# Attention output in transposed form, two heads in the two halves of TensorE's columns, and the softmax transposes one tile later

## The chip, the cores and the metric

The kernel runs on one core of a Trainium2 chip. The metric is device time in microseconds, the median of three runs. The engines spoken of are TensorE (PE; its weight loads are PEld), VectorE (DVE), ScalarE (ACT), GpSimd (POOL) and SyncE's DMA queue (SP).

## The reference, cut to what matters

One encoder block on 1024 tokens of width 1024. The change is inside the attention part; 8 heads of 64 columns each, neighbours of a 16 by 64 grid of tokens:

```python
z = rms_norm(x, norm_mix) @ w_in                      # u | q | k | v
q = rms_norm(q, q_norm) * (HD ** -0.5); k = rms_norm(k, k_norm)
s = einsum('bhcd,bhicjd->bhcij', q_r, k_nb) + bias    # 8 x 16 neighbours
pr = softmax(s);  y_attn = einsum('bhcij,bhicjd->bhcd', pr, v_nb)
x = x + concatenate([y_pool, y_attn]) @ w_out
x = x + expert_choice_ffn(...);  x = x + sigmoid(...) * rms_norm(...)
```

## The kernel before

Tokens are cut into 8 tiles of 128 (eight grid columns by 16 rows), so the neighbours of a tile lie in the tile itself and the ones beside it. Heads are worked in four pairs, 128 columns each. The attention loop runs over 32 tiles t = 8 pr + u, pair after pair. TensorE's order is the order in which the code issues it; in this stretch a scheduler orders the other engines.

`pair_block(t)` is a tile's projection: eight groups of three matmuls (L94, L96, L98 in the helper `mm3`) into `proj`, 384 columns wide. When the eighth is done, ScalarE squares q and k (L307) and copies v (L312), VectorE sums the squares (L309), GpSimd takes the root (L79, L80), and VectorE scales q and k into `qkn` (L313). Between the groups of one tile's projection stand steps of earlier tiles; `side_at(t)` lists them with the group ahead of which each is issued, and 8 means behind the last group:

- step 0: `score(t-3)`, six matmuls of two heads that use the upper and lower 64 rows of the array (L346): q hi and q lo with k hi, then q hi with k lo. VectorE adds the bias and takes the maximum (L351), ScalarE takes the exponential and the row sum (L353).
- steps 5 and 6: `turn_p(t-3, h)`, transposes of head h's exponentials (L361), brought to SBUF as `PT` by ScalarE (head 0) or VectorE (head 1). Step 6 also has `turn_qk(t-1)`, two transposes of `qkn` (L321); ScalarE writes the high part of k and then of q, VectorE the low parts (L327, L328). All tiles of k of a pair are in `kT`.
- steps 7 and 8: `blend(t-3, h)`, attention weights by v in full fp32 (L375): `PT` is the stationary operand, 64 columns of v move. Each such matmul is two instructions on TensorE (176 matmuls are 352 rows of the trace). After head 1 VectorE multiplies with the reciprocal of the row sums (L379, L380) into `ya`, token rows by head columns.

For a tile u the keys reach from tile u-1 to u+1 (`span`), so `score(t-3)` needs the k that `turn_qk(t-2)` writes, except at u = 7, the last tile of a pair.

From tile 4 on, step 3 also holds one piece of the pooling mixer. Weights of the next pair and of `w_out` are loaded and split (L88, L89, L85, L86) along the way. After the 32 tiles, `out_block(u)` multiplies pooling and attention output by `w_out`; it holds the last steps of the attention. `prep(u)` makes its operand `ct`: four transposes of `ya` (L462) into a PSUM buffer of tag t, then a split by ScalarE and VectorE. From block 3 on, the ranking for the experts runs on VectorE. Then 16 experts and a gate, which the change doesn't touch.

Of the kernel before, what the change touches and what calls it, by code (L numbers as in the profile page):

```python
# [10 lines left out]
F32 = mybir.dt.float32  # L11
# [4 lines left out]
ALU = mybir.AluOpType  # L16
# [3 lines left out]
P = 128  # L20
# [3 lines left out]
NU = 8  # L24
# [7 lines left out]
HD = 64  # L32
# [14 lines left out]
def block_kernel(ctx, tc, x, p, vecs, w_u_in, w_qkv, w_pool, bias_rows, w_out, w_router, w_gate, w_up,  # L47
                 w_down, w_ple_gate, w_ple_proj, norm_ffn, norm_ple_post, edge, consts, out):
    nc = tc.nc
    ACT, DVE, POOL, PE, SP = nc.scalar, nc.vector, nc.gpsimd, nc.tensor, nc.sync  # L50
# [8 lines left out]
    def pool(name, bufs, **kw):  # L59
        return tc.tile_pool(name=name, bufs=bufs, reuse_waits="tile", **kw)  # L60

    cp = ctx.enter_context(pool("consts", 1))
    tiny = ctx.enter_context(pool("tiny", 4))
# [4 lines left out]
    ident = cp.tile([P, P], F32, name="ident")  # L68
# [14 lines left out]
    def split(hi, lo, src, gain=None):  # L83
        if gain is None:
            ACT.activation(hi, src, AF.Copy)  # L85
            DVE.tensor_tensor(lo, src, hi.bitcast(F32), op=ALU.subtract)  # L86
            return
        ACT.activation(hi, src, AF.Copy, scale=gain)  # L88
        DVE.scalar_tensor_tensor(lo, src, gain, hi.bitcast(F32), op0=ALU.mult, op1=ALU.subtract)  # L89
# [37 lines left out]
    yas = [rawp["B"].tile([P, 4, 512], F32, tag="raw", name=f"ya_{i}") for i in range(2)]  # L127
# [4 lines left out]
    ps = ps_st.enter_context(pool("ps", 2, space=PSUM))  # L132
# [153 lines left out]
        PE.matmul(pp, w_pool_sb[:, g], Ug, start=True, stop=True)  # L286
        ACT.activation(Ug, pp, AF.Copy, scale=pscale[:, g:g + 1])

    vs, qs, qkns, sbs, PTs, pys, dens = {}, {}, {}, {}, {}, {}, {}
    bias_t = {}  # L290

    def load_bias(pr):
# [38 lines left out]
    def span(u):  # L331
        u0, u1 = max(u - 1, 0), min(u + 2, NU)
        return u0, u1, (u1 - u0) * P

    def score(t):
        pr, u = divmod(t, NU)
        u0, u1, n = span(u)
        b0 = 0 if u == 0 else 5 * P if u == NU - 1 else 2 * P
        q2 = qs[t]
        dens[t] = tiny.tile([P, 2], F32, tag="den", name=f"den_{pr}_{u}")  # L340
        ks = slice(u0 * P, u1 * P)
        pq = [ps.tile([P, 3 * P], F32, tag="s", name=f"s_{pr}_{u}_{h}") for h in range(2)]
        for a, b in ((0, 0), (1, 0), (0, 1)):
            for h in range(2):
                hs = slice(h * HD, (h + 1) * HD)
                PE.matmul(pq[h][:, :n], q2[hs, a], kT[hs, b, ks], start=(a + b == 0), stop=(b == 1))  # L346
        for h in range(2):
            pss = pq[h]
            sb = aw.tile([P, 3 * P], F32, tag="sb", name=f"sb_{pr}_{u}_{h}", bufs=4)
            nmx = tiny.tile([P, 1], F32, tag="nmx", name=f"nmx_{pr}_{u}_{h}")  # L350
            DVE.tensor_tensor_reduce(sb[:, :n], pss[:, :n], bias_t[pr][:, h, b0:b0 + n], -1.0, 3.0e38,  # L351
                                     ALU.add, ALU.min, nmx)
            ACT.activation(sb[:, :n], sb[:, :n], AF.Exp, bias=nmx, scale=-1.0, accum_out=dens[t][:, h:h + 1])  # L353
            sbs[t, h] = sb

    def turn_p(t, h):
# [9 lines left out]
            DVE.tensor_copy(PT[:, :n], pt[:, :n])  # L366
        PTs[t, h] = PT

    def blend(t, h):
        pr, u = divmod(t, NU)  # L370
        u0, u1, n = span(u)
        if h == 0:
            pys[t] = ps.tile([P, 2, HD], F32, tag="py", name=f"py_{pr}_{u}", bufs=1)
        for j in range(u1 - u0):
            PE.matmul(pys[t][:, h], PTs[t, h][:, j * P:(j + 1) * P],  # L375
                      vs[NU * pr + u0 + j][:, h * HD:(h + 1) * HD], start=(j == 0), stop=(j == u1 - u0 - 1))
        if h == 1:
            rd = tiny.tile([P, 2], F32, tag="rd", name=f"rd_{pr}_{u}")
            DVE.reciprocal(rd, dens[t])  # L379
            DVE.tensor_tensor(yas[u // 4][:, u % 4, pr * P:(pr + 1) * P].rearrange("p (a b) -> p a b", b=HD), pys[t],  # L380
                              rd[:, :, None].to_broadcast([P, 2, HD]), op=ALU.mult)

    wo = []

# [13 lines left out]
    NT = 4 * NU  # L398
# [9 lines left out]
    def side_at(t):  # L408
        sides = {}

        def at(i, f, *a):
            sides.setdefault(i, []).append(lambda: f(*a))
        if t == 0:
            at(4, turn_u, NU - 1)
        if t >= 3:
            at(0, score, t - 3)
            at(5, turn_p, t - 3, 0)
            at(6, turn_p, t - 3, 1)
            at(7, blend, t - 3, 0)
            at(8, blend, t - 3, 1)  # L420
        if 1 <= t <= NT:
            at(6, turn_qk, t - 1)
        return sides

    for t in range(NT):
        pr, u = divmod(t, NU)
# [22 lines left out]
    def prep(u):  # L449
        if u == 0:  # L450
            ow.tile([P, 2 * 16], F32, tag="gap", name="gap_ow", bufs=1)
        ct = ow.tile([P, 2, KD, P], F32R, tag="ct", name=f"ct_{u}")
        cts[u] = ct
        for i in range(2):
            usl = Us[i][:, :, PAD:PAD + S].rearrange("p g (r v c) -> p g v r c", v=NU, c=UC)[:, :, u]
            hi = ct[:, 0, 2 * i:2 * i + 2].rearrange("p g (r c) -> p g r c", c=UC)
            lo = ct[:, 1, 2 * i:2 * i + 2].rearrange("p g (r c) -> p g r c", c=UC)
            ACT.activation(hi, usl, AF.Copy)
            POOL.tensor_tensor(lo, usl, hi.bitcast(F32), op=ALU.subtract)
        pt = ps.tile([P, 4, P], F32, tag="t", name=f"yat_{u}", bufs=1)  # L460
        for k in range(4):
            PE.transpose(pt[:, k, :], yas[u // 4][:, u % 4, k * P:(k + 1) * P], ident)  # L462
        split(ct[:, 0, 4:8], ct[:, 1, 4:8], pt)

    def add_x(u, po, j):
        js = slice(j * 512, (j + 1) * 512)
# [199 lines left out]
    def open_route():  # L666
        nonlocal oc, w_r, affq, scr, sel
        oc = ctx.enter_context(pool("oc", 1, side="right"))
        both = oc.tile([P, 2, D], F32, tag="raw", name="both")
        scr, sel = both[:, 0], both[:, 1]  # L670
        w_r = sel[:, 0:KD * E].rearrange("p (k e) -> p k e", e=E)
        SP.dma_start(w_r, w_router[0].rearrange("(k p) e -> p k e", p=P))
        DVE.tensor_tensor(w_r, w_r, gfT[:, :, None].to_broadcast([P, KD, E]), op=ALU.mult)
        affq = sel[:, 128:128 + NU * 32].rearrange("p (u e) -> p u e", e=32)
        POOL.memset(affq, 0.0)
# [72 lines left out]
    load_x(0)  # L748
    load_x(1)
    prep(0)  # L750
    for u in range(NU):
        sides = {}

        def at(i, f, *a):
            sides.setdefault(i, []).append(lambda: f(*a))
        if u == 0:
            at(0, score, NT - 3)
            at(2, turn_p, NT - 3, 0)
            at(2, turn_p, NT - 3, 1)
            at(3, turn_qk, NT - 1)  # L760
            at(4, blend, NT - 3, 0)
            at(4, blend, NT - 3, 1)
            at(4, score, NT - 2)
            at(6, turn_p, NT - 2, 0)
            at(6, turn_p, NT - 2, 1)
            at(6, score, NT - 1)
            at(7, blend, NT - 2, 0)
            at(7, blend, NT - 2, 1)
            at(8, turn_p, NT - 1, 0)
            at(8, turn_p, NT - 1, 1)  # L770
        elif u < NU - 1:
            at(0, norm1, u - 1)
            at(2, turn_x1, u - 1, 0)
            at(2, turn_x1, u - 1, 1)
            at(4, route, u - 1)
        if u == 1:
            at(1, blend, NT - 1, 0)
            at(1, blend, NT - 1, 1)
        if u + 1 < NU:
            at(5, prep, u + 1)  # L780
        if u >= 1 and u + 1 < NU:
            at(0, load_x, u + 1)
        if u == 1:
            def swap():
                att.close()
                open_route()
                rawp["A"] = ctx.enter_context(pool("rawA", NRA, side="right"))
                load_side()
            at(2, swap)
        if u == 2:  # L790
            at(1, split_side, "pT")
            at(4, split_side, "pj")
            at(6, lambda: [load_chunk("A") for _ in range(NRA - 5)])
        if 3 <= u < NU - 1:
            at(6, rank_batch, *((0, 3) if u == 3 else (u - 1, 1)))
            for i in range(8):
                at(i, fill, 8)
        if u == NU - 1:
            at(1, turn_x1, u - 1, 0)
            at(1, turn_x1, u - 1, 1)  # L800
            at(1, norm1, u - 1)
            at(2, logits, u - 1, 0)
            at(3, logits, u - 1, 1)
            at(3, softmax, u - 1)
            at(5, rank_batch, 6, 1)
            for i in range(1, 8):
                at(i, fill, 8)
        run_block(out_block(u), sides)

    u = NU - 1  # L810
# [362 lines left out]
```

## Time and profile before

| | us |
|---|---|
| median of 3 runs | 1684.27 (1682.45 to 1686.49) |
| the profiled execution's own time | 1682.92 |
| its span | 1681.2 |
| TensorE busy | 1630.8 (97%) |
| VectorE busy | 1347.5 (80%) |
| ScalarE busy | 1153.9 (69%) |
| GpSimd busy | 169.1 (10%) |

The page's busy shares are averages over all stages. The attention tiles are the stretch from about 84 to 305 us; the output blocks end at about 437 us; the rest is the experts and the gate.

### The profile page before, as it was taken

To read this page: it belongs to the slowest core of one execution; us is meant where nothing else is said; L and a number is where in the kernel's file an instruction comes from. 1 tells how busy PE (TensorE), PEld (TensorE's weight loads), DVE (VectorE), ACT (ScalarE), POOL (GpSimd) and SP (SyncE) were. 2 spreads that over 40 slices of the span, in tenths; PEclk is the share of its full clock that TensorE was granted. 3 is DMA by queue.
4 is the path that set the end of the run, shared out by engine and by line. 5 is a ranking of instruction groups with operands and counts; after the bars stand their busy time and mean duration, and the time that the engine had idled before them with its cause. 6 is when DMAs were issued, how large, how long until landed. Compare 5 with 4: busy or idle time off the path is not lost.

```text
span 1681.2 us, 22945 instructions
## 1 busy us (share of the span) xinstructions
PE 1630.8 (97%) x8165; PEld 1368.0 (81%) x8165; DVE 1347.5 (80%) x1866; ACT 1153.9 (69%) x1471; POOL 169.1 (10%) x216
## 2 busy tenths in 40 slices
PE   8999998998899999999999999999999999999698
PEld 6889998886778888888888888888888888888587
DVE  4474555459879999999999999999999999999632
ACT  6254554432488888888888888888888888888431
POOL 1111112243310000000000000000000000000100
PEclk9999999999999999999999999999999999999799
DMA  6301201363699999999999999999999999996321
GB/s 187 116 29 33 66 26 51 92 204 97 216 365 373 401 371 400 377 368 408 373 391 385 367 403 377 378 399 369 399 378 367 410 370 392 386 368 242 106 98 59
DMA packets 129266, 470.54 MB, mean 280 GB/s; under 512 B 9600, under 2 KB 14720, under 8 KB 129152
## 3 DMA queue, kind: packets, MB, share of 16 engines
q1 hardware_dynamic: 122848, 445.80, 70.3%
q0 software_dynamic: 6304, 23.28, 5.3%
q8 instruction: 64, 1.05, 0.3%
q14 instruction: 50, 0.41, 0.1%
HBM read 448.00 MB, written 21.04 MB: 279 GB/s over the span
## 4 chain that ended last, share of the span: by engine, by line
PE 84%; DVE 7%; issue 4%; DMA 2%; POOL 1%; ACT 1%; SPq 0%; DVEq 0%; ACTq 0%; POOLq 0%
PE pu L94 7%; PE pu L96 7%; PE pu L98 7%; PE pg L94 6%; PE pg L96 6%; PE pd L96 6%; PE pd L94 6%; PE pg L98 6%; PE pd L98 6%; DVE both L581 3%; PE proj L94 2%; PE proj L98 2%; PE proj L96 2%; PE py L375 2%; PE pq L94 2%
## 5 line engine op out<-in xcount | busy, mean ns | idle before, releaser
L86 DVE TENSOR_TENSOR flo<-fraw,fhi 128x1024 fp32r<-128x1024 f32 x768 | 916.3, 1222 | 71.0 <-ACT fhi L85 33.5
L85 ACT ACTIVATE fhi<-fraw 128x1024 fp32r<-128x1024 f32 x768 | 809.4, 1061 | 192.6 <-PE pd L96 72.6
L94 PE MATMUL pd<-fhi,hidT 128*128 128x512 f32 x512 | 162.1, 398 | 0.0
L94 PE MATMUL pg<-fhi,xeT 128*128 128x512 f32 x512 | 159.2, 392 | 0.7 <-ACT xeT L85 0.7
L94 PE MATMUL pu<-fhi,xeT 128*128 128x512 f32 x512 | 159.2, 392 | 0.0
L96 PE MATMUL pd<-fhi,hidT 128*128 128x512 f32 x512 | 158.4, 390 | 0.0
L98 PE MATMUL pd<-flo,hidT 128*128 128x512 f32 x512 | 158.0, 390 | 0.0
L96 PE MATMUL pu<-fhi,xeT 128*128 128x512 f32 x512 | 158.0, 390 | 0.0
L96 PE MATMUL pg<-fhi,xeT 128*128 128x512 f32 x512 | 157.9, 389 | 0.0
L98 PE MATMUL pg<-flo,xeT 128*128 128x512 f32 x512 | 157.8, 389 | 0.0
L98 PE MATMUL pu<-flo,xeT 128*128 128x512 f32 x512 | 157.6, 389 | 0.0
L98 PEld LDWEIGHTS pd<-flo,hidT 128*128 128x128 f32 x512 | 96.1, 188 | 20.7
L96 PEld LDWEIGHTS pd<-fhi,hidT 128*128 128x128 f32 x512 | 96.1, 188 | 20.6
L96 PEld LDWEIGHTS pg<-fhi,xeT 128*128 128x128 f32 x512 | 96.0, 188 | 20.4 <-DVE xeT L86 0.4
L98 PEld LDWEIGHTS pu<-flo,xeT 128*128 128x128 f32 x512 | 96.1, 188 | 20.3
L96 PEld LDWEIGHTS pu<-fhi,xeT 128*128 128x128 f32 x512 | 96.1, 188 | 20.3
L98 PEld LDWEIGHTS pg<-flo,xeT 128*128 128x128 f32 x512 | 96.1, 188 | 20.1
L94 PEld LDWEIGHTS pg<-fhi,xeT 128*128 128x128 f32 x512 | 94.9, 188 | 19.7 <-ACT xeT L85 1.0
L94 PEld LDWEIGHTS pu<-fhi,xeT 128*128 128x128 f32 x512 | 95.0, 188 | 18.8
L94 PEld LDWEIGHTS pd<-fhi,hidT 128*128 128x128 f32 x512 | 92.8, 188 | 16.6
L994 POOL DMA_INDIRECT acc_rows<-ye,ix x16 | 26.6, 1661 | 764.0 <-ACT ye L993 764.0
L94 PE MATMUL proj<-wph,xT 128*128 128x384 f32 x256 | 99.8, 390 | 0.0
(215 smaller groups left out, 2341.0 us busy)
## 6 DMA issues: line engine op xcount, KB each, us to landing
fraw<-in_w_gate_dram SPq DMA_DIRECT2D x128, 1024.0 KB, 7.2
fraw<-in_w_down_dram SPq DMA_DIRECT2D x128, 1024.0 KB, 9.2
fraw<-in_w_up_dram SPq DMA_DIRECT2D x127, 1024.0 KB, 7.7
x<-in_x_dram SPq DMA_DIRECT2D x15, 512.0 KB, 4.9
wp_raw<-in_w_qkv_dram SPq DMA_DIRECT2D x16, 384.0 KB, 4.6
h_rows<-x POOLq DMA_DIRECT2D x8, 520.5 KB, 4.0
wo_raw<-in_w_out_dram SPq DMA_DIRECT2D x8, 512.0 KB, 3.4
acc_rows<-x SPq DMA_DIRECT2D x8, 512.0 KB, 4.6
```

The lines of the kernel that those rows point to most:

```text
L85: ACT.activation(hi, src, AF.Copy)
L86: DVE.tensor_tensor(lo, src, hi.bitcast(F32), op=ALU.subtract)
L94: PE.matmul(outs[j], xh, wh[j], start=start, stop=False)
L96: PE.matmul(outs[j], xl, wh[j], start=False, stop=False)
L98: PE.matmul(outs[j], xh, wl[j], start=False, stop=stop)
L375: PE.matmul(pys[t][:, h], PTs[t, h][:, j * P:(j + 1) * P], vs[NU * pr + u0 + j][:, h * HD:(h + 1) * HD], start=(j == 0), stop=(j == u1 - u ...
L581: DVE.tensor_tensor(b[:, :, j], a[:, :, 0], a[:, :, 1], op=(ALU.max, ALU.min)[j])
L994: return POOL.indirect_dma_start(out=acc, out_offset=bass.IndirectOffsetOnAxis(ap=idxs[e][:, :1], axis=0), in_=ye, in_offset=None, compute ...
```

## The change

The row sums' reciprocals are taken per head right after the exponentials, and VectorE multiplies the weights with them (128 by up to 384, in SBUF). `blend(t)` now does both heads: 64 columns of v are stationary, 128 columns of `PT` move, head 0 writes PSUM partitions 0 to 63 and head 1 partitions 64 to 127. A copy brings the result to `ya`, which is now head columns by tokens, so `prep` has no transposes and its split reads `ya`. In `side_at`, `turn_p` stands at steps 2 and 3 of tile t for t-4, `blend` at step 6 for t-4, and `turn_qk(t-1)` behind the last group. The list of the output blocks and the point of `swap` are set to match.

```diff
             ACT.activation(sb[:, :n], sb[:, :n], AF.Exp, bias=nmx, scale=-1.0, accum_out=dens[t][:, h:h + 1])
+            rd = tiny.tile([P, 1], F32, tag="rd", name=f"rd_{pr}_{u}_{h}")
+            DVE.reciprocal(rd, dens[t][:, h:h + 1])
+            DVE.tensor_scalar(sb[:, :n], sb[:, :n], rd, None, op0=ALU.mult)
...
-    def blend(t, h):
+    def blend(t):
...
-        if h == 0:
-            pys[t] = ps.tile([P, 2, HD], F32, tag="py", name=f"py_{pr}_{u}", bufs=1)
+        py = ps.tile([P, P], F32, tag="py", name=f"py_{pr}_{u}", bufs=1)
         for j in range(u1 - u0):
-            PE.matmul(pys[t][:, h], PTs[t, h][:, j * P:(j + 1) * P],
-                      vs[NU * pr + u0 + j][:, h * HD:(h + 1) * HD], start=(j == 0), stop=(j == u1 - u0 - 1))
-        if h == 1:
-            rd = tiny.tile([P, 2], F32, tag="rd", name=f"rd_{pr}_{u}")
-            DVE.reciprocal(rd, dens[t])
-            DVE.tensor_tensor(yas[u // 4][:, u % 4, pr * P:(pr + 1) * P].rearrange("p (a b) -> p a b", b=HD), pys[t],
-                              rd[:, :, None].to_broadcast([P, 2, HD]), op=ALU.mult)
+            for h in range(2):
+                hs = slice(h * HD, (h + 1) * HD)
+                PE.matmul(py[hs], vs[NU * pr + u0 + j][:, hs], PTs[t, h][:, j * P:(j + 1) * P],
+                          start=(j == 0), stop=(j == u1 - u0 - 1))
+        DVE.tensor_copy(yas[u // 4][:, u % 4, pr * P:(pr + 1) * P], py)
...
         if t >= 3:
             at(0, score, t - 3)
-            at(5, turn_p, t - 3, 0)
-            at(6, turn_p, t - 3, 1)
-            at(7, blend, t - 3, 0)
-            at(8, blend, t - 3, 1)
-        if 1 <= t <= NT:
-            at(6, turn_qk, t - 1)
+        if t >= 4:
+            at(2, turn_p, t - 4, 0)
+            at(3, turn_p, t - 4, 1)
+            at(6, blend, t - 4)
+        if t >= 1:
+            at(8, turn_qk, t - 1)
...
-        pt = ps.tile([P, 4, P], F32, tag="t", name=f"yat_{u}", bufs=1)
-        for k in range(4):
-            PE.transpose(pt[:, k, :], yas[u // 4][:, u % 4, k * P:(k + 1) * P], ident)
-        split(ct[:, 0, 4:8], ct[:, 1, 4:8], pt)
+        split(ct[:, 0, 4:8], ct[:, 1, 4:8], yas[u // 4][:, u % 4].rearrange("p (k q) -> p k q", q=P))
...
-            at(2, swap)
+            at(3, swap)
```

TensorE at the end of the projection of pair 1, tile 5, before (`proj`, `py`, `s` and `qkt` are PSUM tiles of the projection, the attention output, the scores and the transposes of q and k; `pt` that of the weights; the trailing numbers tell instances apart):

```order
L361 MATMUL pt_2_1_1714<-ident,sb_2_1_1684 128x128 x2
L321 MATMUL qkt_4_1720<-ident,qkn_4_1654 128x128 [waits DVE_49]
L321 MATMUL qkt_4_1720<-ident,qkn_4_1654 128x128
...
L98 MATMUL proj_5_1670<-wpl_3_1233,xT_450 128x384
L375 MATMUL py_2_1731<-v_1_1397,PT_2_1_1718 128x64 [waits DVE_49]
L375 MATMUL py_2_1731<-v_2_1478,PT_2_1_1718 128x64
L375 MATMUL py_2_1731<-v_3_1575,PT_2_1_1718 128x64
L346 MATMUL s_3_0_1756<-kT,q_3_1639 128x384 [waits Activation_49]
L346 MATMUL s_3_1_1757<-kT,q_3_1639 128x384
```

The same place in the changed kernel, from the attention output on:

```order
L379 MATMUL py_1_1746<-PT_1_0_1724,v_0_1315 64x128 [waits Activation_49]
L379 MATMUL py_1_1746<-PT_1_1_1733,v_0_1315 64x128 [waits DVE_49]
L379 MATMUL py_1_1746<-PT_1_0_1724,v_1_1403 64x128
...
L98 MATMUL proj_5_1690<-wpl_3_1233,xT_450 128x384
L321 MATMUL qkt_4_1770<-ident,qkn_4_1672 128x128 x2
L346 MATMUL s_3_0_1780<-kT,q_3_1685 128x384 [waits Activation_49]
L346 MATMUL s_3_1_1781<-kT,q_3_1685 128x384
...
L346 MATMUL s_3_0_1780<-kT,q_3_1685 128x384 [waits DVE_49]
L346 MATMUL s_3_1_1781<-kT,q_3_1685 128x384
```

Before, two groups of the projection and the attention output of two heads stood between the transposes of tile 4's q and k and the scores of tile 3, which read tile 4's k; now the scores follow those transposes directly.

ScalarE at the same place before:

```order
L327 ACTIVATE kT<-qkt_4_1720,vec 128x128 [waits PE_49]
L327 ACTIVATE q_4_1723<-qkt_4_1720,vec 128x128 [waits DVE_49]
L307 ACTIVATE qkn_5_1738<-proj_5_1670,rx 128x256 [waits PE_49]
L312 ACTIVATE v_5_1745<-proj_5_1670,rx 128x128
L353 ACTIVATE sb_3_0_1764,den_3_1755<-sb_3_0_1764,nmx_3_0_1765 128x384 [waits DVE_49,Activation_49]
```

and in the changed kernel:

```order
L307 ACTIVATE qkn_5_1760<-proj_5_1690,rx 128x256 [waits PE_49]
L312 ACTIVATE v_5_1767<-proj_5_1690,rx 128x128
L327 ACTIVATE kT<-qkt_4_1770,vec 128x128 [waits PE_49]
L327 ACTIVATE q_4_1773<-qkt_4_1770,vec 128x128 [waits DVE_49]
L353 ACTIVATE sb_3_0_1788,den_3_1779<-sb_3_0_1788,nmx_3_0_1789 128x384 [waits DVE_49,Activation_49]
```

The write of k's high part, which the scores read, now stands behind the two reads of the projection that has just ended.

VectorE from the maximum over the scores (L351) to the copy of head 1's transposed weights (L366) before:

```order
L351 ISA sb_2_1_1684,nmx_2_1_1685<-s_2_1_1673,bias_882 128x384 [waits PE_49]
L351 ISA nmx_2_1_1685 128x1
L379 RECIPROCAL rd_2_1751<-den_2_1671 128x2 [waits Activation_49]
L366 COPY PT_2_1_1718<-pt_2_1_1714 128x384 [waits PE_49]
L328 SCALAR_TENSOR_TENSOR kT<-qkt_4_1720,vec,kT 128x128 [waits Activation_49]
```

and in the changed kernel, where that copy is L369:

```order
L313 SCALAR_TENSOR_TENSOR qkn_5_1760<-proj_5_1690,rx,qkr_5_1764 128x256 [waits DVE_49,Pool_49]
L328 SCALAR_TENSOR_TENSOR q_4_1773<-qkt_4_1770,vec,q_4_1773 128x128 [waits Activation_49]
L351 ISA sb_3_0_1788,nmx_3_0_1789<-s_3_0_1780,bias_870 128x384 [waits PE_49]
...
L355 RECIPROCAL rd_3_1_1799<-den_3_1779 128x1 [waits Activation_49]
L356 TENSOR_SCALAR sb_3_1_1795<-sb_3_1_1795,rd_3_1_1799 128x384 [waits DVE_49]
L369 COPY PT_2_1_1821<-pt_2_1_1817 128x384 [waits PE_49]
```

The copy of the weights of tile 2 now stands behind the scaling of the weights of tile 3, which waits for their exponentials.

## Rows read from the trace of the kernel before

**Rows 1.** The page, its first part (busy time of TensorE over the span) and the line of its second part with the granted clock of TensorE in 40 slices.

```profile
PE 1630.8 (97%) x8165; PEld 1368.0 (81%) x8165; DVE 1347.5 (80%) x1866; ACT 1153.9 (69%) x1471; POOL 169.1 (10%) x216
...
PEclk9999999999999999999999999999999999999799
```

**Rows 2.** The table by stages: the pair tiles (92 to 312), the output blocks before the ranking (312 to 367), the output blocks with the ranking (367 to 437). Columns: stretch and its length, then busy time and instruction count of PE, PEld, DVE, ACT, POOL, the granted clock, the DMA share, GB/s.

```profile
92.00:312.00 220.00, 211.76 (x1403) 194.27 (x1404) 124.74 (x353) 115.87 (x299) 40.92 (x61) 1.00 0.13 40
312.00:367.00 55.00, 54.98 (x315) 46.51 (x314) 20.80 (x45) 20.64 (x46) 16.75 (x21) 1.00 0.66 200
367.00:437.00 70.00, 60.75 (x319) 50.05 (x320) 64.12 (x303) 16.72 (x44) 23.27 (x29) 1.00 0.37 106
```

**Rows 3.** The timeline of one tile's end and the start of the next, PE, ACT, DVE and POOL. Columns: start in us, duration, engine, line, operation, tiles, shapes, count; in brackets the idle time before it and who ended it.

```profile
186.71 0.38 PE L321 MATMUL qkt<-ident,qkn 128*128 128x128 f32 x2
...
187.13 0.37 ACT L327 ACTIVATE kT<-qkt,vec 128x128 fp32r<-128x128 f32 x1 [0.58 <-PE qkt L321]
187.28 0.33 PE L98 MATMUL proj<-wpl,xT 128*128 128x384 f32 x1
...
187.53 0.35 DVE L328 SCALAR_TENSOR_TENSOR kT<-qkt,vec,kT 128x128 fp32r<-128x128 f32 x1
...
188.04 0.42 PE L94 MATMUL proj<-wph,xT 128*128 128x384 f32 x1
...
188.30 0.34 PE L96 MATMUL proj<-wph,xT 128*128 128x384 f32 x1
...
188.47 0.34 PE L98 MATMUL proj<-wpl,xT 128*128 128x384 f32 x1
...
188.65 0.78 PE L375 MATMUL py<-v,PT 128*128 128x64 f32 x6
188.85 0.47 ACT L307 ACTIVATE qkn<-proj,rx 128x256 f32<-128x256 f32 x1 [0.56 <-PE proj L98]
189.22 0.36 ACT L312 ACTIVATE v<-proj,rx 128x128 f32<-128x128 f32 x1
...
189.35 0.79 PE L346 MATMUL s<-kT,q 64*128 64x384 f32 x6
...
189.67 0.41 DVE L309 TENSOR_REDUCE ssq<-qkn 128x4 f32<-128x256 f32 x1
...
190.08 0.44 PE L94 MATMUL proj<-wph,xT 128*128 128x384 f32 x1
...
190.36 0.34 PE L96 MATMUL proj<-wph,xT 128*128 128x384 f32 x1
...
190.45 1.01 POOL L80 TENSOR_TENSOR qkr<-qkr,neghalf 128x4 f32<-128x4 f32 x1
...
191.49 0.48 DVE L313 SCALAR_TENSOR_TENSOR qkn<-proj,rx,qkr 128x256 f32<-128x256 f32 x1 [0.74 <-POOL qkr L80]
```

**Rows 4.** The timeline at two other tiles: ScalarE's instruction right after a copy of v; then an exponential pair, its accumulator reads, and a transpose that waited for the first of them.

```profile
181.30 0.37 ACT L312 ACTIVATE v<-proj,rx 128x128 f32<-128x128 f32 x1
181.55 0.62 ACT L88 ACTIVATE wph<-wp_raw,vec 128x384 fp32r<-128x384 f32 x1
...
184.06 0.55 DVE L351 CUSTOM_DVE_ANT_0 sb<-s,bias 128x384 f32<-128x384 f32 x1
...
184.71 0.61 ACT L353 ACTIVATE sb<-sb,nmx 128x384 f32<-128x384 f32 x1 [2.04 <-DVE nmx L351]
...
185.23 0.19 ACT L353 ACTIVATION_READ_ACCUMULATOR sb<-sb,nmx 128x1 f32 x1
185.33 0.60 ACT L353 ACTIVATE sb<-sb,nmx 128x384 f32<-128x384 f32 x1
...
185.47 0.55 PE L361 MATMUL pt<-ident,sb 128*128 128x128 f32 x3 [0.78 <-ACT sb L353]
...
185.83 0.18 ACT L353 ACTIVATION_READ_ACCUMULATOR sb<-sb,nmx 128x1 f32 x1
```

**Rows 5.** The waits of TensorE from 60 to 312: who waited for whom, us in total, times, the longest.

```profile
PE pt L361 <- ACT sb L353: 7.2, 7, 2.0
PE qkt L321 <- DVE qkn L313: 2.7, 2, 1.4
```

**Rows 6.** The groups of instructions by shape, 92 to 312: count | busy us, mean ns of one | idle before.

```profile
L366 DVE COPY PT<-pt 128x384 f32<-128x384 f32 x22 | 12.2, 556 | 16.4 <-PE pt L361 16.4
...
L89 DVE SCALAR_TENSOR_TENSOR wpl<-wp_raw,vec,wph 128x384 fp32r<-128x384 f32 x20 | 11.8, 613 | 1.5 <-ACT wph L88 1.5
...
L86 DVE TENSOR_TENSOR wol<-wo_raw,woh 128x1024 fp32r<-128x1024 f32 x6 | 7.3, 1219 | 0.4 <-PE proj L98 0.4
...
L379 DVE RECIPROCAL rd<-den 128x2 f32<-128x2 f32 x29 | 4.8, 165 | 18.6 <-ACT sb L353 18.6
```

**Rows 7.** The chain of waits, pieces in order of time: start us, us on the chain, what. First a pair of 128x512 products in full fp32 between rows of the projection, then eight 128x128 transposes.

```profile
199.91 0.86 PE pool L286 x2
...
330.08 0.87 PE x1t L504 x8
```

**Rows 8.** TensorE's timeline in the output blocks: a wait in the first block, the transposes of one tile of attention output, and a wait in the ranking.

```profile
307.90 0.47 PE L94 MATMUL po<-woh,ct 128*128 128x512 f32 x1 [1.45 <-DVE qkn L313]
...
364.89 0.60 PE L462 MATMUL yat<-ident,ya 128*128 128x128 f32 x4
...
383.86 0.28 PE L590 MATMUL at<-ident,both 128*32 128x128 f32 x1 [2.54 <-DVE ct L86]
```

More of the change, by code (lines that the diff above doesn't have):

```diff
@@ L287, in pool_mix @@
         ACT.activation(Ug, pp, AF.Copy, scale=pscale[:, g:g + 1])
-    vs, qs, qkns, sbs, PTs, pys, dens = {}, {}, {}, {}, {}, {}, {}
+    vs, qs, qkns, sbs, PTs, dens = {}, {}, {}, {}, {}, {}
     bias_t = {}
@@ L757, in block_kernel @@
             at(0, score, NT - 3)
[L758 to L765, printed above, removed]
+            at(1, turn_p, NT - 4, 0)
+            at(1, turn_p, NT - 4, 1)
+            at(2, turn_qk, NT - 1)
+            at(3, blend, NT - 4)
+            at(3, score, NT - 2)
+            at(4, turn_p, NT - 3, 0)
+            at(4, turn_p, NT - 3, 1)
+            at(6, blend, NT - 3)
             at(6, score, NT - 1)
[L767 to L770, printed above, removed]
+            at(7, turn_p, NT - 2, 0)
+            at(7, turn_p, NT - 2, 1)
         elif u < NU - 1:
@@ L776, in block_kernel @@
         if u == 1:
-            at(1, blend, NT - 1, 0)
-            at(1, blend, NT - 1, 1)
+            at(1, blend, NT - 2)
+            at(1, turn_p, NT - 1, 0)
+            at(1, turn_p, NT - 1, 1)
+            at(3, blend, NT - 1)
         if u + 1 < NU:
```

## The prediction

> **What bounds the kernel now.** I read the page first: TensorE is busy for 1630.8 of 1681.2 us and its clock is at the upper of its two levels, 2.4 GHz, in all but one slice [rows 1]. The table by stages then tells the stages apart [rows 2]. In the pair tiles TensorE is busy for 211.8 of 220 us, VectorE for 124.7, ScalarE for 115.9: TensorE's own order is the bound there, and what that order waits for. In the first output blocks it is full as well (54.98 of 55 us). In the blocks with the ranking VectorE is the bound (64.1 of 70 us) and TensorE waits for it, as at 383.86 [rows 8]; what TensorE is spared there is worth nothing. The experts behind are not touched. So the change has to be costed in TensorE's time from tile 0 to block 3, and the span moves with that.
>
> The timeline of a steady tile gives the prices [rows 3]. The projection issues a matmul every 0.17 us. I call the start of a tile's last projection matmul (188.47) T; the second matmul of the next tile starts at 190.36, 1.89 us later. With nothing between, it would be 0.35. A head's attention output costs 187.28 to 188.30 less 0.35, 0.67 us for six instructions, so the scores cost 1.89 - 0.35 - 0.67 = 0.87.
>
> **The change, part by part.**
>
> *Attention output.* Before: 352 instructions of 0.67/6 = 0.111 us, 39.1 us. Now there are as many, with 128 columns moving. Two fp32 products of 512 columns take 0.86 us [rows 7], so 128 columns take 0.43/4 = 0.107. The trace of before has no product in half the array's columns. The nearest row is the scores, which use half of the rows for each head: six of them would take 6 x 0.174 = 1.04 us one after another and take 0.87, so the two heads run together, three times 0.174 = 0.52, and 0.35 us goes for entering and leaving that mode. I take the same here. Each product is two instructions on one half, then two on the other, so the halves overlap one instruction late: seven slots of 0.107 for twelve instructions, five for the eight of an edge tile. That is 24 x 7 + 8 x 5 = 208 slots, 22.3 us, and 32 modes at 0.35, 11.2 us: 33.5, a gain of 5.6. The ends: no overlap at all, 352 x 0.107 + 11.2 = 48.9, a loss of 9.8; full overlap and no price for the mode, 176 x 0.107 = 18.8, a gain of 20.3.
>
> The Trainium skill, TensorEngine Tiling (Array Packing), section Key Properties, says that a change of the tiling mode, unlike one of the tile, drains TensorE, and its Performance Considerations count on up to twice the speed for a stationary operand of 64 columns. The first speaks against this change, and the 0.35 us at the scores agrees with it; without a drain the part above would gain 11.2 us more. No run here shows the second for columns yet.
>
> *Transposes of `ya`.* Eight transposes take 0.87 us [rows 7], so the four of a tile take 0.44 us [rows 8]. Block 0's lie beside a wait of 1.45 us for the scaled q and k [rows 8], those of blocks from 4 on in the ranking: four count, -1.8. What hides the others is VectorE in the ranking; its own split of `ct` stays.
>
> *Weights a tile later.* TensorE waited 7.2 us in seven places for exponentials [rows 5]. They are now transposed a whole tile after their scores: -7.2. The first transposes of q and k waited 2.7 us in two places [rows 5] and stand behind two more groups, 6 x 0.174 = 1.04 us each: -2.1.
>
> *The new wait for k.* The scores of tile t-3 read the k of t-2, whose transposes now end right before them. ScalarE's queue has two reads of the projection ahead of that k (the order of ScalarE above). From [rows 3, 4]: the square starts 0.38 behind T, the copy of v 0.37 later, the next instruction 0.25 after a copy of v, so k's high part runs from T + 1.00 to 1.37. TensorE starts 0.05 after ScalarE's end (185.42 to 185.47): scores at T + 1.42, next tile's second matmul 1.01 later (189.35 to 190.36), T + 2.43. Without a wait that would be 0.35 + 2 x 0.109 for the transposes + 0.87 = T + 1.44. The price is 0.99 us. k's low part, on VectorE 0.03 after the high one and 0.35 long [rows 3], is there at T + 1.75, before the last pair of scores wants it at about T + 1.9. Scores issued in tiles 3 to 31 are 29; those of the three last tiles of a pair among them have their k a tile earlier: 26 x 0.99 = +25.7. The thirtieth, in block 0, lies beside the wait of 1.45. In three tiles a split of `w_out`, 1.22 us [rows 6], stands ahead of the row of squares and k's low part on VectorE, which then comes at 0.38 + 1.22 + 0.41 + 0.35 = T + 2.36, 0.47 late; in two a split of the next pair's weights, some 0.6 us [rows 6], precedes the square on ScalarE: +2.6 in all.
>
> *Scaling the weights.* VectorE gets a reciprocal (0.165 us [rows 6]) and a multiply for each of 64 heads and tiles. No row shows such a multiply: 0.17 is the lower end (the reciprocal), 0.61 the upper (a two-input operation on 128 x 384 [rows 6]); I take 0.4, as it has one wide input. VectorE has room for it, but in 14 of the pair tiles the copy of head 1's weights is queued behind both multiplies (VectorE's order above), and `blend` waits for that copy. Scaled q and k start at T + 0.88 + 1.82 = 2.70 (189.67 to 191.49 [rows 3]); the maximum follows at about 3.4; from there 0.65 to the first exponential and 1.30 to the end of the second sum (184.06, 184.71, 186.01 [rows 4]) give 5.35; with 0.03 + 0.17 + 0.4 + 0.56 [rows 6] the copy ends at T + 6.5. TensorE wants it at 2.43 + 16 x 0.174 + 6 x 0.109 + 0.21 = T + 6.1. That is 0.4 x 14 = +5.6; the ends are 0.2 and 0.6, +2.8 and +8.4.
>
> *At nothing.* The copy in place of the multiply on the way to `ya` leads only to `prep`, a stage later. `swap` one group later issues four loads later on SP; GpSimd already waits for one of them, TensorE for none before the end of the blocks. If that cover were gone it would cost one group, 1.4 us.
>
> Sum: -5.6 - 1.8 - 7.2 - 2.1 + 25.7 + 2.6 + 5.6 = +17.2. Against the profiled execution's own 1682.9 us that is 1700.1; the median of the runs is 1.35 above that execution, so 1701.
>
> **The rivals.** *The halves don't run together* (the change doesn't do what it says): 15.4 us more than my term, 1717. For it: no row of columns; against it: the scores' rows do run together. *Column halves are no mode and overlap fully*, 14.6 us less: 1687, within 0.2% of before and so not slower. For it: all 128 rows stay in use, as in the projection around it; against it: the 0.35 us at the scores. It is decided at 0.64 us for a tile's attention output; at 1.05 or above, my forecast stands. *ScalarE gets to k sooner*: k's copy started 0.42 us after its transposes where nothing stood ahead (186.71 to 187.13 [rows 3]); then the scores start at T + 0.17 + 0.42 + 0.37 + 0.05 = 1.01, the wait is 0.58 and the time 1691. Against it: the queue's order. Below a wait of 0.33 us the kernel would be no slower.
>
> **How the numbers follow.** My forecast has 0.55, 1701 give or take 4. The first rival has 0.17, the second 0.12, the third 0.10, and 0.06 is left for gains by which the kernel comes out below 1681. About 0.2% of the time, 3.4 us, is what a measurement can tell from no change. Slower by more takes the forecast, the first and the third rival, 0.82; the second is "same", 0.12; faster 0.06. The range reaches from 1686, just below the second, to 1718, just above the first.
>
> **What would show it.** In the changed profile: the waits of TensorE should list scores waiting for ScalarE's k (L327), some 26 times, about 1 us each, 25 us in all, and no more waits of the weights' transposes for exponentials; the attention output's wait for head 1's copy (L369) a few tenths, some 14 times; two instructions of different heads starting nearly together in the attention output, about 1.05 us for twelve. I'm wrong if the wait for k is under 0.4 us, or if the twelve take 0.7 or 1.6.

## The result and the profile after

The changed kernel takes 1703.62 us (median of 4 runs, 1700.63 to 1704.94) against 1684.45 us of the kernel before (4 runs, 1682.45 to 1686.49): ratio 1.0109, 95% interval 1.0097 to 1.0121. It is slower by 19 us; 1701 was forecast. Its profiled execution took 1704.25 us, with a span of 1702.5.

The page's first line answers to [rows 1], and says as little about the place as that did: TensorE's busy time is 2.5 us longer, its span 21.3.

```profile
PE 1633.3 (96%) x8133; PEld 1349.8 (79%) x8133; DVE 1372.8 (81%) x1962; ACT 1146.5 (67%) x1471; POOL 164.4 (10%) x216
```

The table by stages says where: in the 220 us of pair tiles TensorE is busy for 195.81 us where it was for 211.76 [rows 2], with 1287 instructions instead of 1403. It has got less done since it stands idle.

```profile
92.00:312.00 220.00, 195.81 (x1287) 162.70 (x1286) 129.93 (x399) 99.17 (x272) 32.46 (x54) 0.99 0.12 39
```

The timelines of both kernels give the same by difference. From the first to the last projection matmul, before took 67.34 to 303.89 us, 236.6; after takes 67.72 to 325.06, 257.3: 20.8 of the 21.3 us. From there to the last matmuls of the output blocks it is 129.3 before and 129.4 after, so behind the pair tiles nothing was lost and nothing gained.

What TensorE waits for from tile 0 to the last pair, in place of [rows 5] (who waited for whom, us in total, times, the longest):

```profile
PE s L346 <- ACT kT L327: 23.9, 27, 1.3
PE s L346 <- DVE kT L328: 5.1, 5, 2.5
PE py L379 <- DVE PT L369: 0.9, 1, 0.9
...
PE qkt L321 <- DVE qkn L313: 0.3, 1, 0.3
```

The waits for exponentials have gone, and the scores wait for k's high part in 27 places: 26 of the pair tiles and the first output block. One tile's end, answering to [rows 3] (start, duration, engine, line, operation, tiles, shapes, count; in brackets the idle time and who ended it):

```profile
199.69 0.34 PE L98 MATMUL proj<-wpl,xT 128*128 128x384 f32 x1
...
199.96 0.88 PE L379 MATMUL py<-PT,v 128*64 128x128 f32 x12
...
201.05 0.34 PE L96 MATMUL proj<-wph,xT 128*128 128x384 f32 x1
...
201.74 0.34 PE L98 MATMUL proj<-wpl,xT 128*128 128x384 f32 x1
...
201.93 0.38 PE L321 MATMUL qkt<-ident,qkn 128*128 128x128 f32 x2
202.12 0.47 ACT L307 ACTIVATE qkn<-proj,rx 128x256 f32<-128x256 f32 x1 [4.11 <-PE proj L98]
202.50 0.36 ACT L312 ACTIVATE v<-proj,rx 128x128 f32<-128x128 f32 x1
...
202.75 0.37 ACT L327 ACTIVATE kT<-qkt,vec 128x128 fp32r<-128x128 f32 x1
...
203.17 0.82 PE L346 MATMUL s<-kT,q 64*128 64x384 f32 x6 [0.86 <-ACT kT L327]
...
204.20 0.34 PE L96 MATMUL proj<-wph,xT 128*128 128x384 f32 x1
```

Read it from T = 201.74. Square at +0.38, copy of v at +0.76, k's high part at +1.01, scores at +1.43, the next tile's second matmul at +2.46. The forecast had 0.38, 0.75, 1.00, 1.42 and 2.43. The twelve instructions of the attention output take 201.05 - 199.69 = 1.36 us, less 0.35 for two matmuls of the projection with nothing between: 1.01, where 1.05 was forecast.

Two things in this profile were not forecast. In the first output block the scores wait 1.94 us more, for k's low part:

```profile
325.43 0.69 DVE L86 TENSOR_TENSOR wol<-wo_raw,woh 128x512 fp32r<-128x512 f32 x1 [0.96 <-PE proj L98]
...
328.23 0.48 DVE L313 SCALAR_TENSOR_TENSOR qkn<-proj,rx,qkr 128x256 f32<-128x256 f32 x1 [1.18 <-POOL qkr L80]
328.63 0.34 DVE L328 SCALAR_TENSOR_TENSOR kT<-qkt,vec,kT 128x128 fp32r<-128x128 f32 x1
...
329.03 0.69 PE L346 MATMUL s<-kT,q 64*128 64x384 f32 x2 [1.94 <-DVE kT L328]
```

VectorE has the scaling of q and k (L313) ahead of k's low part, and that scaling stands still until GpSimd has the root. Where a weight split (L86) delays VectorE, the low part falls behind that round trip through GpSimd.

And TensorE's granted clock, before 1.00 in every such stretch from 60 to 430 us, drops in some (10 us each: TensorE's busy time, count, granted clock, DMA share, GB/s):

```profile
80.00:90.00 10.00, 6.84 (x31) 0.83 0.16 50
...
190.00:200.00 10.00, 8.46 (x46) 0.83 0.55 184
...
320.00:330.00 10.00, 7.18 (x49) 0.92 0.00 1
330.00:340.00 10.00, 9.88 (x47) 0.74 0.67 157
```

A mean of 0.83 is a third of the stretch at 1.2 GHz instead of 2.4. Ahead of the drop in 190 to 200 the scores of a tile with weight splits had waited twice (1.34 us at 193.17, 0.20 at 193.99). Ahead of the two others scores had waited for k's low part, 1.94 us at 329.03 and 2.51 in the first tile, where VectorE had two weight splits and two steps of the pooling mixer ahead of it:

```profile
85.64 0.38 PE L346 MATMUL s<-kT,q 64*128 64x256 f32 x2 [2.51 <-DVE kT L328]
```

### The profile page after: what moved, and what is told of

Read it like the earlier page. It is cut to its first block, busy times and chain, and to the rows that moved or that the text cites. A ratio compares the mean times of both kernels' runs of the same rounds, so it can differ in the third digit from the quotient of the medians.

```text
span 1702.5 us, 22855 instructions
## 1 busy us (share of the span) xinstructions
PE 1633.3 (96%) x8133; PEld 1349.8 (79%) x8133; DVE 1372.8 (81%) x1962; ACT 1146.5 (67%) x1471; POOL 164.4 (10%) x216
## 3 DMA queue, kind: packets, MB, share of 16 engines
q8 instruction: 64, 1.05, 0.3%
## 4 chain that ended last, share of the span: by engine, by line
PE 82%; DVE 8%; issue 4%; DMA 2%; ACT 2%; POOL 1%; SPq 0%; DVEq 0%; POOLq 0%; ACTq 0%
PE pu L94 7%; PE pu L96 7%; PE pu L98 7%; PE pg L94 6%; PE pg L96 6%; PE pd L96 6%; PE pd L94 6%; PE pg L98 6%; PE pd L98 6%; PE proj L94 3%; DVE both L578 2%; PE proj L98 2%; PE proj L96 2%; PE pq L94 2%; PE pq L96 2%
## 5 line engine op out<-in xcount | busy, mean ns | idle before, releaser
L86 DVE TENSOR_TENSOR flo<-fraw,fhi 128x1024 fp32r<-128x1024 f32 x768 | 916.2, 1221 | 71.0 <-ACT fhi L85 35.0
L94 PEld LDWEIGHTS pu<-fhi,xeT 128*128 128x128 f32 x512 | 94.9, 188 | 18.8
```

Of the source, the lines that this page charges most:

```text
L94: PE.matmul(outs[j], xh, wh[j], start=start, stop=False)
```

## The experiments

All are compared with the changed kernel's 1703.62 us and with the kernel before, which ran in each set (1685.06 to 1685.63 us, median). The changed kernel ran in the first set alone, where before took 1684.45, so differences of a microsecond or two between sets show nothing.

| run | us (median) | ratio to before, 95% |
|---|---|---|
| e1_qk_step5 | 1673.16 | 0.9915 to 0.9945 |
| e2_head_by_head | 1707.67 | 1.0115 to 1.0153 |
| e3_no_scaling | 1700.64 | 1.0074 to 1.0106 |
| e4_turn_p_back | 1692.00 | 1.0031 to 1.0059 |
| e5_one_half | 1718.95 | 1.0186 to 1.0216 |
| e6_before_qk8 | 1718.68 | 1.0180 to 1.0206 |
| e7_blend_by_scores | 1664.78 | 0.9865 to 0.9894 |
| e8_turn_p_back_qk6 | 1692.59 | 1.0024 to 1.0050 |
| e9_k_first | 1692.87 | 1.0032 to 1.0057 |
| e10_back_no_scaling | 1674.01 | 0.9912 to 0.9945 |
| e11_blend7 | 1667.92 | 0.9876 to 0.9908 |
| e12_before_tile_later | 1677.53 | 0.9944 to 0.9973 |

### Is the wait for k the loss?

**e1.** One line of `side_at`:

```diff
-            at(8, turn_qk, t - 1)
+            at(5, turn_qk, t - 1)
```

> The transposes of q and k stand behind the fifth group of the projection and no longer right before the scores; all else is the changed kernel. Theory (the scores' wait for k is the loss): the 25 to 28 us of waits for k's two parts go, and nothing takes their place, since the fifth group comes about 4.7 us behind T, by which time the scaled q and k are there in nearly all tiles; 1703.6 - 25 to 28 gives 1675 to 1679, below both kernels, and the seam of a tile's end falls from 2.46 to about 1.25 us. Rival (TensorE would have lost that time anyway, to the column mode, the later weights or a clock that falls): 1695 or more, with waits of the same sum under another name.

1673.16 us, 30.5 less than the changed kernel and 12 less than before. TensorE's waits are then:

```profile
PE qkt L321 <- DVE qkn L313: 4.3, 5, 1.8
PE po L94 <- DVE qkn L313: 1.8, 1, 1.8
```

No scores are among them. Other waits did take the place of some: these rows and three smaller ones sum to 8.6 us, where the changed kernel's waits sum to 30.9. What was gained beyond that difference lies in large part in the clock, which is 1.00 in every 10 us stretch from 60 to 350 (by an estimate from the rows of those stretches, 10 us times what each lacks to 1.00, it cost the changed kernel up to 7 us there). The first output block waits 1.8 us instead of 0.86 + 1.94. That position alone decided whether the change was a gain or a loss.

**e9.** The square, the copy of v and the scaling are issued in code behind `turn_qk`, by a function at step 8:

```diff
             at(8, turn_qk, t - 1)
+        at(8, finish, t)
```

> The changed kernel with the work on a finished projection (square, copy of v, scaling of q and k) written behind the transposes of q and k. On ScalarE the copy of v then stands behind k's high part; the square still stands ahead of it. The transposes stay right before the scores. Theory (the scores wait for k because ScalarE's queue has other reads ahead of it): k's high part starts at the end of the square, T + 0.75 instead of T + 1.00, the scores 0.25 us earlier, 26 x 0.25 = 6.5 us: 1695 to 1699, and the wait at the clean seams falls from 0.86 to about 0.6. Rival (the delay lies between the transposes' end and ScalarE, whatever stands in its queue): 1702 to 1706.

1692.87 us, 10.7 less than the changed kernel. The same place in the tile:

```profile
196.89 0.34 PE L98 MATMUL proj<-wpl,xT 128*128 128x384 f32 x1
...
197.26 0.47 ACT L314 ACTIVATE qkn<-proj,rx 128x256 f32<-128x256 f32 x1 [2.42 <-PE proj L98]
197.64 0.36 ACT L335 ACTIVATE kT<-qkt,vec 128x128 fp32r<-128x128 f32 x1
...
198.05 0.89 PE L354 MATMUL s<-kT,q 64*128 64x384 f32 x6 [0.60 <-ACT kT L335]
```

(Lines are shifted by eight.) k's high part starts at T + 0.75 and the wait is 0.60, both as forecast. So at the clean seams the queue at ScalarE sets the wait, not the transposes' own latency. The seams (the tiles' ends with transposes and scores, 29 in all) take 5.4 us less together; the rest lies in the clock, which is 1.00 in the stretches in which the changed kernel's fell, and in the first output block. There another part of the edit counts: on VectorE k's low part now stands ahead of the scaling (318.67 and 320.16 us), and the wait of 1.94 us is gone.

**e6.** The kernel before, with `at(6, turn_qk, t - 1)` at step 8.

> The kernel before with one edit: the transposes of q and k stand behind the last projection group and the second head's attention output, so right before the scores. Theory (the scores wait for k since ScalarE has the square and the copy of v ahead of it; the price is what is left of that path when TensorE gets there): the transposes start 0.84 us behind T instead of 0.17, k's high part runs from T + 1.26 to 1.63, the scores start at 1.68 instead of 1.15: a wait of some 0.5 us 26 times, 13 us, less 2 us of the first transposes' own waits: 1694 to 1700. Rival 1 (the wait is not what the changed kernel lost its time to): 1682 to 1688. Rival 2 (the price is a fixed 1 us wherever the two stand together): 1708 or more.

1718.68 us: the theory's sum was wrong, and the first rival too. The time is the second rival's, but not its reason, as TensorE's waits show:

```profile
PE s L346 <- ACT kT L327: 12.3, 26, 0.6
PE s L346 <- DVE kT L328: 9.2, 6, 2.5
```

The 26 waits for ScalarE are the 13 us of the theory, at 0.5 us each. Besides, six tiles wait 9.2 us for k's low part. One of them, in VectorE's rows:

```profile
200.83 0.61 DVE L89 SCALAR_TENSOR_TENSOR wpl<-wp_raw,vec,wph 128x384 fp32r<-128x384 f32 x1
...
202.61 0.48 DVE L313 SCALAR_TENSOR_TENSOR qkn<-proj,rx,qkr 128x256 f32<-128x256 f32 x1 [1.18 <-POOL qkr L80]
203.01 0.34 DVE L328 SCALAR_TENSOR_TENSOR kT<-qkt,vec,kT 128x128 fp32r<-128x128 f32 x1
...
203.41 0.44 PE L346 MATMUL s<-kT,q 64*128 64x384 f32 x2 [1.84 <-DVE kT L328]
```

It is the round trip through GpSimd of the changed kernel's first output block, again behind a weight split. And the clock falls, in the two stretches below and in those from 90 to 110, 130 to 140 and 330 to 350 us:

```profile
80.00:90.00 10.00, 6.85 (x30) 0.76 0.19 63
...
200.00:210.00 10.00, 7.57 (x40) 0.83 0.46 157
```

In the profiled execution (1714.30 us, below the median) the transposes of q and k, the scores and what stands beside them cost 27 us more than before, measured from the start of the last projection matmul ahead to that of the second one behind: 0.57 us each 26 times, 15 us, as the theory had it, and 12 more in the six tiles that wait for k's low part. The projection's own matmuls take some 5 us more, at the lower clock. So the order "transposes of q and k, then scores" costs more than its mean wait, in tiles in which weight splits or the pooling mixer hold up VectorE. The theory had no term for that, and the prediction too small a one. What part of the 12 us is the clock and what part the wait was not tested by itself.

### Do the two halves of the columns run together?

**e2.** The loops of `blend` swapped, heads outside, keys inside.

> The attention output's products of head 0 are all issued before those of head 1, so that no two neighbours on TensorE but the pair in the middle lie in different halves of the array; the number of instructions and the mode are the same. Theory (two halves of columns run together when their instructions alternate): twelve instructions go from 1.01 to about 12 x 0.107 + 0.35 = 1.63 us, 24 x 0.62 + 8 x 0.4 = +18 us, 1719 to 1722. Rival (they don't run together, and the 1.01 us come from short instructions): unchanged, 1702 to 1706.

1707.67 us, 4 more; twelve instructions take 1.27 us (from 199.10 to 200.72 in its timeline, less 0.35), and neither expectation holds. The run was no control: head 1's first instruction started before the last of head 0's, so the halves still ran together in part. It needed one half for both heads.

**e5.**

```diff
-        py = ps.tile([P, P], F32, ...)
+        py = ps.tile([P, 2, P], F32, ...)
...
+                PE.matmul(py[0:HD, h], vs[NU * pr + u0 + j][:, hs], PTs[t, h][:, j * P:(j + 1) * P],
...
+        for h in range(2):
+            DVE.tensor_copy(yas[u // 4][h * HD:(h + 1) * HD, u % 4, pr * P:(pr + 1) * P], py[0:HD, h])
```

> Both heads' attention output goes into the same half of the array's columns, head 0's products before head 1's, and two copies instead of one move it to the place where head 1's half would have stood; the count of instructions and the mode are those of the changed kernel. The run with head 0's products ahead of head 1's in two halves was no proof without overlap, since there head 1's first instruction started while four of head 0's were still to come. Theory (halves run together, and one half alone can't): twelve instructions take 12 x 0.107 + 0.35 = 1.63 us and eight 1.21, against 1.01 and 0.79; 21 x 0.62 + 7 x 0.42 = 16 us, less some 3 of waits for head 1's weights that this hides: 1714 to 1720. Rival (instructions run together in one half too, the gain came from shorter instructions): 1702 to 1708.

1718.95 us, 15.3 more than the changed kernel. Twelve instructions take 205.32 - 203.32 - 0.35 = 1.65 us:

```profile
203.32 0.34 PE L98 MATMUL proj<-wpl,xT 128*128 128x384 f32 x1
203.59 1.52 PE L379 MATMUL py<-PT,v 128*64 128x128 f32 x12
...
205.32 0.34 PE L96 MATMUL proj<-wph,xT 128*128 128x384 f32 x1
```

Less the 0.35 us of the mode, one half takes 1.30 and two take 0.66, a factor of 1.97: the halves run together without a slot lost. The Trainium skill, TensorEngine Tiling (Array Packing), section Theoretical Speedup, gives up to 2 for a dimension of 64; the trace agrees.

### What do the scaled weights and the tile's delay cost and give?

**e3.** The three lines of the reciprocal and the multiply left out of the changed kernel.

> The reciprocal and the multiply of the weights on VectorE are left out, so the attention output is not divided by the sum of the exponentials; all else is the changed kernel. Theory (the multiply delays head 1's copy of the weights by some 0.3 to 0.4 us in the tiles where the attention output waits for it): 3 to 8 us less, 1696 to 1701, with the waits of the attention output gone and those of the scores for k as they were. Rival (VectorE has room, the multiply is hidden): within 2 us of 1703.6. A gain of over 10 us would say that VectorE's queue also holds up k's low part.

1700.64 us, 3.0 less, the lower end of what was expected. The two ratios' intervals overlap (1.0097 to 1.0121 and 1.0074 to 1.0106), so the times alone don't exclude the rival; the traces speak against it. The attention output of the same tile, in the changed kernel and in e3:

```profile
180.95 1.20 PE L379 MATMUL py<-PT,v 128*64 128x128 f32 x12
```

```profile
180.80 0.88 PE L376 MATMUL py<-PT,v 128*64 128x128 f32 x12
```

Eight such places take 1.23 to 1.51 us in the changed kernel and 1.00 in e3 (worked out as the 1.01 above); over the 28 tiles up to the last projection the attention output takes 30.8 and 28.3 us, 2.5 less. The list of waits doesn't show it: its one wait of 0.9 us for the copy of head 1's weights stands in e3 as well, so "the waits of the attention output gone" didn't come true there.

**e4** puts the weights' transposes back where they were before, and those of q and k ahead of the fifth group:

```diff
-            at(2, turn_p, t - 4, 0)
-            at(3, turn_p, t - 4, 1)
-            at(6, blend, t - 4)
-            at(8, turn_qk, t - 1)
+            at(5, turn_p, t - 3, 0)
+            at(6, turn_p, t - 3, 1)
+            at(8, blend, t - 3)
+            at(4, turn_qk, t - 1)
```

> The order of before (transposes of the weights behind groups 5 and 6 of the tile that scores them, those of q and k behind group 4) with the transposed attention output and the scaled weights of the changed kernel. Theory (a tile's delay spares TensorE 7.2 us of waits for exponentials and 2 us for the first q and k, and the multiply lengthens those waits by 0.4 us each): 8 to 14 us above the first kernel of this set, 1684 to 1692. Rival (the delay isn't needed): equal to the first of this set within 2 us, 1673 to 1680.

1692.00 us, 18.8 above e1 and so more than expected. **e8** is e4 with `turn_qk` at step 6, as in the kernel before.

> The order of before for the transposes of the weights, as in the run that had them back, but the transposes of q and k behind the sixth group, where the kernel before had them, and not behind the fourth. Theory (that run's 18.8 us more than the best one were two things: 10 us of waits of the transposes of q and k, which were put too early there, and 13 us of waits for exponentials and scaled weights, less 5 us of a mode shared): without the first, 1682 to 1686. Rival (all of it is the weights): 1689 to 1693.

1692.59: the theory of two separate parts fell. The waits, e4's first and then e8's:

```profile
PE pt L364 <- DVE rd L355: 9.9, 17, 1.5
PE qkt L321 <- DVE qkn L313: 7.8, 6, 2.3
PE qkt L321 <- ACT U L287: 5.7, 8, 1.6
PE pt L364 <- DVE sb L356: 2.6, 3, 1.1
```

```profile
PE pt L364 <- DVE rd L355: 17.6, 17, 2.7
PE pt L364 <- DVE sb L356: 5.2, 6, 2.1
PE qkt L321 <- DVE qkn L313: 2.7, 2, 1.4
```

Both sum to some 26 us. Where TensorE no longer waits for q and k, it waits as much longer for the scaled weights: in that order the chain from scores to transposes sets the tile. **e10** is e8 without the scaling.

> The run with the order of before for the transposes of the weights and those of q and k behind the sixth group, with the reciprocal and the multiply of the weights left out, so the attention output is not divided by the sum of the exponentials. Theory (in that order the chain from the scores over the exponentials to the transposes is as long as a tile, and the multiply on it lengthens the tile): TensorE's waits for the weights fall from 22.8 us to the 7 to 10 us of the kernel before, 1692.6 - 13 to 16: 1676 to 1680. Rival (the multiply is not on it; the transposes wait for the exponentials as before and the rest is a clock or the column mode): 1689 to 1693.

1674.01 us, 18.6 less than e8. The weights' waits are what they were in [rows 5]:

```profile
PE pt L361 <- ACT sb L353: 7.3, 6, 2.1
```

**e12** moves the weights' transposes and the attention output a tile later in the kernel before, and nothing else.

> The kernel before with its own attention output (two heads one after the other, scaled at the end, its result transposed later), but the transposes of the weights and the attention output a tile later, with the out blocks' list shifted alike; the transposes of q and k stay behind the sixth group. It tells what the later weights give alone. Theory (TensorE's 7.2 us of waits for exponentials go, and nothing comes for it): 1677 to 1680. Then the transposed output in the best order, at 1664.8, is worth another 12 to 15 us: the two heads beside the scores cost 1.73 us where 0.67 + 1.53 stood, 21 x 0.47 + 7 x 0.23 = 11.5, and the transposes of ya. Rival (the delay gave the best version all it has): 1663 to 1667.

1677.53 us, 7.5 less than before. The delay is worth 7.5 us by itself, and 27.8 (e8 to e7, which differ in nothing else of weight) once the scaling is on the chain; part of that is the clock, which is 0.83 or 0.84 in three of the 10 us stretches of the pair tiles in e8 and in one in e7.

### The best order

**e7.** e1 with two steps changed, `at(8, blend, t - 4)` and `at(6, turn_qk, t - 1)`.

> The version with the transposes of q and k taken away from the scores, with two more moves: the attention output stands behind the last group, right before the scores, and the transposes of q and k behind the sixth. Theory (entering and leaving a mode costs about 0.35 us, and a neighbour in another tiling shares part of it; the attention output's waits for head 1's weights end): the run with the old order shows 1.72 us for the two together against 1.00 + 0.92 apart, 28 x 0.2 = 5.6 us, and some 4 us of waits for weights and 2 for q and k go: 1661 to 1666. Rival (the modes cost the same side by side, and the waits come back under another name): 1670 to 1675.

1664.78 us, 20 less than before and 39 less than the changed kernel. **e11** takes `blend` back by one group, to step 7.

> The best version so far (attention output right before the scores, transposes of q and k behind the sixth group) with the attention output one group earlier, so that a group of the projection lies between it and the scores; nothing else. Theory (neighbours in the two tilings share part of the price of entering and leaving a mode): 20 x (1.00 + 0.92 - 1.73) + 7 x (0.79 + 0.92 - 1.52) = 5 us more, 1669 to 1672. Rival (what made that version faster was the time that the weights' copies got): 1664 to 1667.

1667.92, 3.1 above e7, somewhat under the 5 expected. A tile of e7, then the two pieces apart in e11:

```profile
224.96 0.34 PE L98 MATMUL proj<-wpl,xT 128*128 128x384 f32 x1
225.23 0.88 PE L379 MATMUL py<-PT,v 128*64 128x128 f32 x12
226.04 0.79 PE L346 MATMUL s<-kT,q 64*128 64x384 f32 x6
...
227.04 0.34 PE L96 MATMUL proj<-wph,xT 128*128 128x384 f32 x1
```

```profile
219.92 0.33 PE L98 MATMUL proj<-wpl,xT 128*128 128x384 f32 x1
...
221.27 0.34 PE L96 MATMUL proj<-wph,xT 128*128 128x384 f32 x1
221.44 0.33 PE L98 MATMUL proj<-wpl,xT 128*128 128x384 f32 x1
...
222.72 0.34 PE L96 MATMUL proj<-wph,xT 128*128 128x384 f32 x1
```

Together 2.08 - 0.35 = 1.73 us; apart 1.00 + 0.93. Two tilings side by side spare 0.20 us of entering and leaving.

## Why the prediction was right

The time and the main mechanism, the wait for k, were right. Of the smaller terms four were off by some 2 to 3 us each, and TensorE's clock had none; that they cancelled to within 3 us was luck. Sums over tiles are worked out as in the text above, from the start of the last matmul ahead to the second one behind, less 0.35.

- **The new wait for k, +25.7 and +2.6.** Right in place and cause, and in size at the clean seams: 0.97 us (2.46 - 0.35 - 0.22 for the transposes - 0.92 for the scores, as e1 has them alone) against 0.99, in 26 tiles. Four tiles with a weight split are 0.44 to 0.91 us longer than the clean ones, 2.5 in all, where 2.6 was forecast. All 29 seams together take 63.3 us; with the scores and transposes as e1 has them apart (25.4 + 29 x 0.22) they would take 32. So 31 us were lost against 28; the 3 us are two early tiles in which the pooling mixer's steps on VectorE delay k's low part (the first with its wait of 2.51 us above), and the term had left the mixer out. e1 and e9 show the cause; the third rival (ScalarE gets to k sooner) has fallen.
- **Attention output, -5.6.** The overlap is shown by e5, so the rivals of no overlap and of no price for the mode have fallen: twelve and eight instructions differ by two slots, 1.01 - 0.79 = 2 x 0.11, and six slots off 1.01 leave 0.35 for the mode. Its size was underrated: the halves start together, so twelve instructions are six slots and not seven (1.01 us, against 1.05) and eight are four and not five (0.79, against 0.89); 24 x 1.01 + 8 x 0.79 = 30.6, a gain of 8.5.
- **Scaling the weights, +5.6.** The multiply takes 0.418 us (0.4 estimated), but 8 tiles wait for it and not 14, some 0.3 us each: 2.5 us by the traces, 3.0 by the times of e3. What the term missed is that the tile's delay is what makes the scaling cheap: without it, it costs 18.6 (e8, e10).
- **Weights a tile later, -7.2; first q and k, -2.1.** Right: those waits are gone or 0.3 us, and e12 gives 7.5 for the delay.
- **Transposes of `ya`, -1.8, and the scores in block 0 "beside the wait of 1.45".** The second is wrong: those scores wait 0.86 and 1.94 us themselves, 1.4 more than the wait beside which they were to lie. With the clock at 0.92 and 0.74 in 320 to 340 us (up to 3 us, estimated as in e1) that took up the gain: from the last projection to the end of the output blocks it is 129.4 us against 129.3. In e1, where those scores don't wait and the clock stays at 1.00, it is 124.6. That the transposes' part of it is 1.8 no run shows by itself.
- **Not in the sum: TensorE's clock.** The drops in the pair tiles cost some 3 us in slower projections and transposes (0.32 us a matmul instead of 0.17 while the clock was low).

With what was measured the pair tiles come to -8.5 + 31 + 2.5 - 7.2 - 2.4 + 3 = +18.4, where the trace has +20.8. Two losses that are no part of these terms fill the gap to within half a microsecond: the attention output waits 1.8 us in places where it waits in e3 too, 1.4 of it in one tile behind a split of `w_out`, and one product of the pooling mixer comes 1.0 us late.

## What to carry to other kernels

An instruction's place in TensorE's order should be read against the queue of the engine that brings its operand, not against that engine's busy share: here three groups of the projection between the transposes and their reader were worth 30 us. A step that adds work to a chain and a step that gives the chain more time should be costed as a pair, since either alone gives another sign. When an idea comes bundled with a new order, try the idea in the old order and the order without the idea; here the idea was worth 11.6 us (e10, without its scaling, against before) to 12.8 (e7 against e12) and one misplaced step hid it.

## What the runs showed of the hardware

- Products in the two halves of the columns run together even when they are not issued in alternation: in program order head by head, twelve take 1.27 us, between 1.01 (alternating) and 1.65 (one half).
- Going from one tiling straight to another costs less than going back to the full array between them, by 0.20 us here (e7, e11).
- TensorE's granted clock fell to 1.2 GHz for a few us after waits of 1.34, 1.94 and 2.51 us in the changed kernel. It stayed at 1.00 in e9 after a wait of 1.76 us, and in the kernel before after one of 2.0. What decides was not isolated.
